# Two pairs of down blocks in each half by seven products of halves, and the output stored by fours of blocks

## The chip, the core and the metric

The kernel runs on one core of a Trainium2 chip. The metric is the device time of one execution in microseconds. The core's engines are named as in the profile: PE (matrix products) with PEld (its weight loads), DVE (vector operations), ACT (activations, scaling, casts), POOL (a second, slower vector engine, which here also issues some of the loads) and SP (which issues most loads and the stores).

## The reference

One layer of a decoder, for 256 prompt tokens and 8 sampled ones: half a SwiGLU block, a mixing block (a group of mLSTM heads beside a group of short convolutions), half a SwiGLU block, and a last norm.

```python
D_MODEL, SEQ, DEC_BATCH, D_FF = 2048, 256, 8, 5504

def swiglu(x, wg, wu, wd):
    return (jax.nn.silu(x @ wg) * (x @ wu)) @ wd

h = h + 0.5 * swiglu(rmsnorm(h, norm_ffn1), ffn1_gate, ffn1_up, ffn1_down)
h = h + mixing_block(rmsnorm(h, norm_mix), ...)
h = h + 0.5 * swiglu(rmsnorm(h, norm_ffn2), ffn2_gate, ffn2_up, ffn2_down)
y = rmsnorm(h, norm_final)
```

The change is in the products with `ffn1_down` and `ffn2_down` (5504 x 2048 each) and in how `y` leaves the chip.

## The kernel before

Tokens lie along the columns: all T = 264 of them, as 16 blocks `h[kb]` of 128 channels x 264. Every weight is cut into blocks of 128 x 128. Full precision is got from half-size numbers: a weight `w` becomes `hi + lo`, an activation likewise, and each block product is three matmuls, hi with hi, hi with lo, lo with hi (`three`, L287 to L289). `high` (ACT, L220) rounds to the high part, `low` (DVE, L228) takes what is left.

Weights are streamed in the order of one list, `weight_plan`. `fetch` takes the next chunk of up to 8 blocks: SP loads it into `wraw`, ACT writes `whi`, DVE writes `wlo`. `product` consumes the chunks in order and keeps AHEAD = 5 of them fetched. With `lag` set, the `low` of a chunk is issued only when the next chunk is fetched, so that DVE doesn't wait for ACT.

A SwiGLU layer (`ffn`) runs in two halves of the inner dimension, 22 and 21 blocks of 128. In each half come first the gate and up products of its blocks (16 k-blocks each), which leave the activations `act[j]` as high and low parts, then 16 down products (22 or 21 k-blocks), whose sums DVE adds to `h` (L846). After the second half of a layer each finished `h[db]` goes to `done`: in layer 1 that cuts it into parts for the mixing block and squares it, in layer 2 it squares it and applies the last gain. The squares (`square`) run on POOL.

Some gate/up blocks (`SEVEN`: 11 in layer 1, 12 in layer 2) go by seven products of halves. The two output blocks (gate and up), the two halves of the 16 k-blocks and the two halves of the tokens make a 2 x 2 by 2 x 2 product, for which seven products and some sums do in place of eight. One such pair costs

- four half loads of raw weights (`load`, issued by POOL, two buffers `sraw`), 
- the parts of three blocks as they are (`blocks` on ACT, `blocks_low` on DVE, tiles `sa`) and of four sums of blocks (`all_sums`, `sums_low`, tiles `sb`; three additions on DVE into `ssum`, L355 to L357),
- sums of the activations, the "forms" (`form` on POOL, `form_split` on ACT and DVE), made once for all pairs of a layer,
- 7 x 8 x 3 = 168 matmuls over 132 columns (`chunk_by_seven`, L409) in two chunks: three products, then four,
- the putting together of the results by DVE (`by_seven`, L759 to L763).

The preparation of the next pair is spread in eight steps over the ordinary products between two pairs (`prepare_step`, called after each chunk; `step_end` holds it back). `at(n, fn)` puts work off by n products (half products too): `tick` counts them. All engines take their instructions in the order in which the program issues them.

At the end the last two down blocks are made in two spans of tokens (136, then 128 columns), so that the first span's output is normed and stored while PE works on the second. `scaled` multiplies two blocks of `h` by the norm (L902) and stores them (L903). `watch` keeps sums of absolute values of the results, `judge_early` and `judge_late` compare them with bounds, and if one is outside, a branch repeats the whole step in full precision.

Of the kernel before, what the change touches and what calls it, by code (L numbers as in the profile page):

```python
# [8 lines left out]
F32 = mybir.dt.float32  # L9
# [40 lines left out]
SEVEN = {n: list(range(j, 22, 3)) + list(range(22, NFB, 3)) for n, j in (("1", 10), ("2", 7))}  # L50
PAIRS = sum(len(v) for v in SEVEN.values())
TH = T // 2
# [29 lines left out]

def weight_plan(a, apart=None):
# [10 lines left out]
    def ffn(layer, first):  # L94
        gu, d = a[f"w{layer}gu"], a[f"w{layer}d"]
        for half, blocks in enumerate(HALVES):
            for j in blocks:
                if j >= first and (apart is None or j not in apart[layer]):
                    add((layer, "g", j), gu[j, 0], KB)
                    add((layer, "u", j), gu[j, 1], KB)  # L100
            for db in range(KB):
                b0, b1 = blocks[0], blocks[-1] + 1
                add((layer, "d", half, db), d[db][:, b0:b1, :], b1 - b0)
# [42 lines left out]
def step(ctx: ExitStack, tc: tile.TileContext, a: dict, shared, bad=None):  # L146
# [7 lines left out]
    AHEAD = 5 if half_size else 2  # L154
    queue = nc.gpsimd if half_size else nc.sync
# [12 lines left out]
    hpair = []  # L168
    for kb in range(0, KB, 2):
        t = hpool.tile([128, 2, T], F32, name=f"h{kb}", tag=f"h{kb}")  # L170
        hpair.append(t)
        h += [t[:, 0, :], t[:, 1, :]]
# [144 lines left out]
    def prepare(pool, layer):  # L317
# [3 lines left out]
        gu = a[f"w{layer}gu"]  # L321
# [4 lines left out]

        def load(j, c):
            raws[c] = raw = pool.tile([128, 4, 4, 128], F32, tag="raw", name="sraw", bufs=2)
            for g in range(2):
                blocks = gu[j, g].rearrange("p (s k) m -> p s k m", s=2)  # L330
# [14 lines left out]
        sums = [None]  # L345

        def all_sums(j, c):
            raw = raws[c]
            if c == 0:
# [4 lines left out]
            sums[0] = s = pool.tile([128, 4, 4, 128], F32, tag="ssum", name="ssum")  # L354
            nc.vector.tensor_tensor(s[:, 2], raw[:, 2], raw[:, 3], op=ALU.add)  # L355
            nc.vector.tensor_tensor(s[:, 3], s[:, 2], raw[:, 1], op=ALU.subtract)
            nc.vector.tensor_tensor(  # L357
                s[:, 0:2], raw[:, 0:4:2],
                s[:, 3].unsqueeze(1).to_broadcast([128, 2, 4, 128]), op=ALU.subtract,
            )  # L360
            high(formed[j, 1][0][:, :, ks[c]], s, sw)

        def sums_low(j, c):
            hi, lo = formed[j, 1]
            low(lo[:, :, ks[c]], sums[0], hi[:, :, ks[c]], sw)

        for n, j in enumerate(SEVEN[layer]):
# [5 lines left out]
            for c in range(2):  # L373
                s = -4 if n == 0 else 8 * n + (-2, -1)[c]
# [8 lines left out]
    def chunk_by_seven(j, c, x, forms, banks):  # L383
# [3 lines left out]
        hi, lo = formed.pop((j, c))  # L387
        p, q, r = banks
        left, right = slice(0, TH), slice(TH, T)

        def form(n):
# [4 lines left out]
            (p, 1, lambda k: x[k][:, :, left]), (p, 0, lambda k: x[k + 8][:, :, left]),  # L396
            (r, 0, form(3)),
        )
        if c == 1:

            work = (
                (q, 0, lambda k: x[k][:, :, right]), (q, 2, form(1)), (q, 1, form(0)),
                (p, 2, form(2)),
            )
        for f, (ps, col, b) in enumerate(work):
# [7 lines left out]
            if f == 1:  # L413
# [157 lines left out]
    def judge(x, bounds):  # L571

        n = x.shape[-1]
        ok = tmp.tile([128, NSTAT], F32, tag="ok", name="ok", bufs=1)[:, :n]
# [50 lines left out]

    class Norm:
# [10 lines left out]
        def cut(self, kb):  # L637
# [10 lines left out]
            else:  # L648
                split(x, h[kb], gain)
# [3 lines left out]
        def form(self, k):  # L653


            b = tmp.tile([128, 7, TH], F32, tag="y7", name="form_b", bufs=1)
            t = tmp.tile([128, 4, TH], F32, tag="form_t", name="form_t", bufs=2)
# [5 lines left out]
            side.tensor_tensor(t[:, 0:2], b[:, 1:4:2], b[:, 0:2], op=ALU.subtract)  # L663
            side.tensor_tensor(t[:, 2], b[:, 3], t[:, 0], op=ALU.subtract)
            side.tensor_tensor(t[:, 3], t[:, 2], b[:, 2], op=ALU.subtract)
            self.parts = t

        def form_split(self, k):
            t = self.parts
            x = self.fpool.tile([128, 2, 4, TH], PART, tag=f"f{k}", name=f"f{k}")  # L670
            high(x[:, 0], t)
            self.forms.append(x)
            at(0.5 if seq[0] == int(seq[0]) else 1, low, x[:, 1], t, x[:, 0])
# [992 lines left out]
```

## Time and profile before

| | |
|---|---|
| median of 3 runs | 1816.19 us (1815.84 to 1818.47) |
| profiled execution | 1816.65 us; its span 1814.9 us |
| PE busy | 1797.8 us, 17918 matmuls |
| DVE busy | 1388.2 us, 2141 instructions |
| ACT busy | 953.1 us, 1329 instructions |
| POOL busy | 237.2 us, 338 instructions |
| granted clock of PE | 0.998 |
| moved by DMA | 381.34 MB |

The four down stages lie at about 243 to 362, 581 to 694, 1349 to 1468 and 1687 to 1786 us. In the timeline, times are counted from the start of the span. A row of a group gives its line, engine and operation, what it writes and reads, the shape, the count, then the busy time, the mean of one in ns, and the idle time of the engine before it with what ended it. In a row of a window the first number behind the colon is its length, then come the busy times.

### The profile page before, as it was taken

To read this page: it belongs to the slowest core of one execution; us is meant where nothing else is said; L and a number is where in the kernel's file an instruction comes from. 1 tells how busy PE (TensorE), PEld (TensorE's weight loads), DVE (VectorE), ACT (ScalarE), POOL (GpSimd) and SP (SyncE) were. 2 spreads that over 40 slices of the span, in tenths; PEclk is the share of its full clock that TensorE was granted. 3 is DMA by queue.
4 is the path that set the end of the run, shared out by engine and by line. 5 is a ranking of instruction groups with operands and counts; after the bars stand their busy time and mean duration, and the time that the engine had idled before them with its cause. 6 is when DMAs were issued, how large, how long until landed. Compare 5 with 4: busy or idle time off the path is not lost. (4 is left out here: it accounts for less than half of the span.)

```text
span 1814.9 us, 42526 instructions
## 1 busy us (share of the span) xinstructions
PE 1797.8 (99%) x17918; PEld 1591.0 (88%) x17918; DVE 1388.2 (76%) x2141; ACT 953.1 (53%) x1329; POOL 237.2 (13%) x338
## 2 busy tenths in 40 slices
PE   9999999999999999999999999999999999999997
PEld 7889988899998888888888888899988889999886
DVE  7888975579997657788888766789986459998564
ACT  7664554445554444567566645655554335554442
POOL 0310000000100222222121022410000001010110
PEclk9999999999999999999999999999999999999999
DMA  8665666645654565888887655756567646564553
GB/s 301 243 222 168 219 208 230 203 153 189 215 192 153 185 193 189 302 284 276 280 283 238 222 180 185 254 191 220 191 193 249 199 148 215 191 207 153 191 186 101
DMA packets 118615, 381.34 MB, mean 210 GB/s; under 512 B 15084, under 2 KB 24908, under 8 KB 118416
## 3 DMA queue, kind: packets, MB, share of 16 engines
q1 hardware_dynamic: 95952, 302.29, 50.1%
q0 software_dynamic: 21504, 75.81, 12.2%
q8 instruction: 142, 2.33, 0.5%
q10 hardware_dynamic: 960, 0.45, 0.1%
q14 instruction: 57, 0.47, 0.1%
HBM read 366.72 MB, written 11.78 MB: 209 GB/s over the span
## 5 line engine op out<-in xcount | busy, mean ns | idle before, releaser
L228 DVE SCALAR_TENSOR_TENSOR wlo<-wraw,whi 128x1024 f16<-128x1024 f32 (+2 forms) x600 | 688.2, 1172 | 103.5 <-ACT whi L220 102.9
L220 ACT ACTIVATE whi<-wraw 128x1024 f16<-128x1024 f32 (+2 forms) x600 | 580.0, 1000 | 160.6 <-PE ps L288 140.7
L289 PE MATMUL ps<-x,wlo 128*128 128x264 f16 x1952 | 538.8, 276 | 1.1 <-DVE wlo L228 1.1
L287 PE MATMUL ps<-x,whi 128*128 128x264 f16 x1952 | 538.8, 276 | 0.2 <-ACT whi L220 0.2
L288 PE MATMUL ps<-x,whi 128*128 128x264 f16 x1952 | 538.8, 276 | 0.0
L289 PEld LDWEIGHTS <-wlo 128*128 128x128 f16 x4522 | 442.5, 98 | 67.4 <-DVE wlo L228 2.4
L288 PEld LDWEIGHTS <-whi 128*128 128x128 f16 x4522 | 442.4, 98 | 66.2
L287 PEld LDWEIGHTS <-whi 128*128 128x128 f16 x4522 | 442.7, 98 | 65.6 <-issue 0.6
L289 PE MATMUL ps<-a,wlo 128*128 128x264 f16 (+2 forms) x1418 | 382.7, 273 | 0.4 <-DVE wlo L228 0.4
L287 PE MATMUL ps<-a,whi 128*128 128x264 f16 (+2 forms) x1418 | 382.8, 273 | 0.0
L288 PE MATMUL ps<-a,whi 128*128 128x264 f16 (+2 forms) x1418 | 382.8, 273 | 0.0
L287 PE MATMUL ps<-xm,whi 128*128 128x264 f16 x896 | 247.3, 276 | 0.0
L289 PE MATMUL ps<-xm,wlo 128*128 128x264 f16 x896 | 247.3, 276 | 0.0
L288 PE MATMUL ps<-xm,whi 128*128 128x264 f16 x896 | 247.3, 276 | 0.0
L220 ACT ACTIVATE sb<-ssum 128x2048 f16<-128x2048 f32 x46 | 87.9, 1911 | 181.2 <-DVE ssum L357 181.2
L409 PEld LDWEIGHTS <-sb 128*128 128x128 f16 x2208 | 128.8, 98 | 0.7
L846 DVE SCALAR_TENSOR_TENSOR h<-ps,h 128x264 f32<-128x264 f32 x62 | 26.7, 431 | 126.7 <-PE ps L289 126.7
L228 DVE SCALAR_TENSOR_TENSOR sb<-ssum,sb 128x2048 f16<-128x2048 f32 x46 | 105.2, 2288 | 8.0 <-ACT sb L220 5.6
L409 PE MATMUL ps<-f,sb 128*128 128x132 f16 x1656 | 99.0, 221 | 0.0
L409 PEld LDWEIGHTS <-sa 128*128 128x128 f16 x1656 | 97.1, 98 | 0.7
L331 POOL DMA_DIRECT2D sraw<-in_w2gu x48 | 34.6, 723 | 420.7 <-issue 371.5
L228 DVE SCALAR_TENSOR_TENSOR sa<-sraw,sa 128x1536 f16<-128x1536 f32 x46 | 81.8, 1778 | 3.1
(255 smaller groups left out, 1601.7 us busy)
## 6 DMA issues: line engine op xcount, KB each, us to landing
wraw<-in_w2gu SPq DMA_DIRECT2D x124, 512.0 KB, 4.6
wraw<-in_w1gu SPq DMA_DIRECT2D x120, 512.0 KB, 4.8
wraw<-in_win SPq DMA_DIRECT2D x112, 512.0 KB, 5.7
wraw<-in_w1d SPq DMA_DIRECT2D x80, 448.0 KB, 4.0
wraw<-in_w2d SPq DMA_DIRECT2D x80, 448.0 KB, 4.1
sraw<-in_w2gu POOLq DMA_DIRECT2D x48, 512.0 KB, 4.9
sraw<-in_w1gu POOLq DMA_DIRECT2D x44, 512.0 KB, 5.3
wraw<-in_wout SPq DMA_DIRECT2D x32, 512.0 KB, 4.8
```

The source lines that it names most:

```text
L220: nc.scalar.activation(dst, src, AF.Copy, scale=scale)
L228: nc.vector.scalar_tensor_tensor(dst, src, scale, hi, op0=ALU.mult, op1=ALU.subtract)
L287: nc.tensor.matmul(ps, wh, xk[:, 0, :], start=first, stop=False)
L288: nc.tensor.matmul(ps, wh, xk[:, 1, :], start=False, stop=False)
L289: nc.tensor.matmul(ps, wl, xk[:, 0, :], start=False, stop=last)
L331: queue.dma_start(raw[:, 2 * g : 2 * g + 2], blocks[:, :, ks[c], :])
L409: nc.tensor.matmul(out, w[:, f, k, :], b(k)[:, part, :], start=(k + term == 0), stop=(k == 7 and term == 2),)
L846: nc.vector.scalar_tensor_tensor(h[db], ps, 0.5 / (sw * sa[layer]), h[db], op0=ALU.mult, op1=ALU.add)
```

## The change

In each half of each layer the down blocks 6 and 7, and 10 and 11, go by sevens over the first 16 of the half's 22 or 21 k-blocks; the other 6 or 5 k-blocks of each are an ordinary product ("rest"). The order is written by `down_order`: ordinary products 0 to 5, then for a pair first chunk, an ordinary block, the first rest, second chunk, an ordinary block, the second rest.

Forms of the activations are made anew in each half: POOL adds the high and low parts of each block and makes three subtractions, ACT and DVE split the result. They start in the half's last gate/up block. The preparation of weights is paused from there until down block 3. The sums of weights are made in the buffers of the raw weights instead of `ssum`, and the load of the second half of the next pair is issued one step later. The down stages run with `lag` set.

The low parts of normed blocks (but of the first norm and the last block) are put off by one product. `judge_early` moves behind the last pair. The output is scaled and stored by four blocks, the last four by two and two: 4 stores for the first span and 5 for the second, where there were 8 and 8. Some temporary buffers change their pools or share one.

```diff
+SEVEN_DOWN = {"1": ((3, 5), (3, 5)), "2": ((3, 5), (3, 5))}
+def down_order(pairs, n):
+    order = []
+    for p in range(-(-n // 2)):
+        if p in pairs:
+            for c in range(2):
+                order += [("seven", p, c), ("one", 2 * p + 2 + c), ("rest", 2 * p + c)]
+        elif p - 1 not in pairs:
+            order += [("one", db) for db in range(2 * p, min(2 * p + 2, n))]
+    return order
...
@@ prepare
+            cut = slice(blocks_[0], blocks_[0] + KB)
+            for p in SEVEN_DOWN[layer][half]:
+                jobs.append((("d", half, p), d[2 * p][:, cut], d[2 * p + 1][:, cut]))
...
-            sums[0] = s = pool.tile([128, 4, 4, 128], F32, tag="ssum", name="ssum")
-            nc.vector.tensor_tensor(s[:, 2], raw[:, 2], raw[:, 3], op=ALU.add)
-            nc.vector.tensor_tensor(s[:, 3], s[:, 2], raw[:, 1], op=ALU.subtract)
+            nc.vector.tensor_tensor(raw[:, 3], raw[:, 2], raw[:, 3], op=ALU.add)
+            nc.vector.tensor_tensor(raw[:, 1], raw[:, 3], raw[:, 1], op=ALU.subtract)
             nc.vector.tensor_tensor(
-                s[:, 0:2], raw[:, 0:4:2],
-                s[:, 3].unsqueeze(1).to_broadcast([128, 2, 4, 128]), op=ALU.subtract,
+                raw[:, 0:4:2], raw[:, 0:4:2],
+                raw[:, 1].unsqueeze(1).to_broadcast([128, 2, 4, 128]), op=ALU.subtract,
             )
-            high(formed[j, 1][0][:, :, ks[c]], s, sw)
+            high(formed[j, 1][0][:, :, ks[c]], raw, sw)
...
-                s = -4 if n == 0 else 8 * n + (-2, -1)[c]
+                s = -4 if n == 0 else 8 * n + (-2, 0)[c]
...
+            def form(k):
+                b = form_blocks()
+                for n, i in enumerate((k + 8, k)):
+                    y = act[blocks[i]]
+                    side.tensor_tensor(
+                        b[:, 2 * n : 2 * n + 2].rearrange("p s t -> p (s t)"), y[:, 0, :],
+                        y[:, 1, :], op=ALU.add,
+                    )
+                forms.append(form_sums(b))
...
+                    if downs and j == blocks[-1]:
+                        paused, step_end[0] = step_end[0], min(step_end[0], step_no[0] + 1)
+                        for k in range(9):
+                            when = 2 + int(1.5 * k) / 2
+                            if k:
+                                at(when, form_split, k - 1)
+                            if k < 8:
+                                at(when, form, k)
...
+                def down_by_seven(p):
+                    y, halves = assemble(seven.pop(p))
+                    def summed():
+                        both = hpair[p].rearrange("p i t -> p (i t)")
+                        nc.vector.scalar_tensor_tensor(
+                            both, y[:, 0:4].rearrange("p s t -> p (s t)"), scale, both,
+                            op0=ALU.mult, op1=ALU.add,
+                        )
+                    at(1, halves)
+                    at(1, summed)
+                for kind, db, *c in down_order(downs, KB - apart):
+                    if kind == "seven":
+                        if c[0] == 0:
+                            seven[db] = [bank() for _ in range(3)]
+                        chunk_by_seven(("d", half, db), c[0], x, forms, seven[db])
+                        if c[0] == 1:
+                            down_by_seven(db)
+                        continue
+                    if downs and db == 3:
+                        step_end[0] = paused
+                    over = range(KB if kind == "rest" else 0, len(x))
+                    ps = product((layer, "d", half, db), x, over)
...
-        at(2 * NFB + 2 * KB - 8, judge_early)
+        more = 2 * sum(len(p) for p in SEVEN_DOWN["2"])
+        at(2 * NFB + 2 * KB + more - 2, judge_early)
...
-    for i in range(1 + half_size, NP):
-        scaled(i, cols, queues[i])
+    for k0, n, dma in ((8, 4, nc.sync), (12, 2, nc.scalar), (14, 2, nc.sync)):
+        scaled(k0, n, cols, dma)
```

More of the change, by code (lines that the diff above doesn't have):

```diff
@@ L325, in prepare @@
         step_no[0] = None
+        step_end[0] = 9
         def load(j, c):
@@ L648, in cut @@
             else:
-                split(x, h[kb], gain)
+                high(x[:, 0, :], h[kb], gain)
+                later = self.col != V_N1 and kb < KB - 1
+                (lambda *f: at(1, *f) if later else f[0](*f[1:]))(
+                    low, x[:, 1, :], h[kb], x[:, 0, :], gain
+                )
             self.x[kb] = x
@@ L662, in form @@
                 )
[L663 to L666, printed above, removed]
+            self.parts = form_sums(b)
         def form_split(self, k):
[L669 to L673, printed above, removed]
+            self.forms.append(form_parts(self.fpool, f"f{k}", self.parts))
         def square(self, kb):
```

151 lines of the change are left out of this document (94 added, 57 removed).

## The prediction

> **What bounds the kernel now.** I read the page first, then the list of waits on PE, then single stretches of the timeline, then the groups by shape.
>
> ```profile
> span 1814.9 us, 42526 instructions
> PE 1797.8 (99%) x17918; PEld 1591.0 (88%) x17918; DVE 1388.2 (76%) x2141; ACT 953.1 (53%) x1329; POOL 237.2 (13%) x338
> PEclk9999999999999999999999999999999999999999
> PE ps L962 <- DVE ok L956: 2.0, 1, 2.0
> PE ps L289 <- DVE wlo L228: 1.5, 3, 1.1
> ```
>
> PE is busy for 1797.8 of 1814.9 us at full granted clock, and the waits on it that the profile can name are one of 2.0 us at the very end and a few of about 1 us or less. So the time is the sum of the pitches of 17918 matmuls plus some 17 us of start, end and small gaps. Work on another engine costs nothing until it starves PE. The question is then what a matmul costs at the two widths involved: 264 columns in an ordinary product, 132 in a product by sevens.
>
> ```profile
> 27.91 0.28 PE L287 MATMUL ps<-x,whi 128*128 128x264 f16 x1
> ...
> 38.60 0.28 PE L289 MATMUL ps<-x,wlo 128*128 128x264 f16 x1
> ...
> 211.54 2.92 PE L409 MATMUL ps<-x,sa 128*128 128x132 f16 x48
> 214.30 1.54 PE L409 MATMUL ps<-f,sa 128*128 128x132 f16 x24
> 215.68 0.28 PE L287 MATMUL ps<-x,whi 128*128 128x264 f16 x1
> ```
>
> The first two rows are the first and last of 96 matmuls in a row: (38.60 - 27.91) / 95 = 112.5 ns from start to start (the 0.28 in a row is the latency of one, not its pitch). The last three hold 72 narrow ones between 211.54 and 215.68: 4.14 / 72 = 57.5 ns, with no gap where the width changes. Each has its own weight load, as the equal counts of PE and PEld on the page say.
>
> **The change, PE.** Sixteen of a half's 22 or 21 k-blocks of two output blocks cost 2 x 16 x 3 = 96 wide matmuls, 96 x 112.5 ns = 10.80 us. By sevens they are 7 products x 8 k-blocks x 3 terms = 168 narrow ones, 168 x 57.5 ns = 9.66 us. The "rest" products keep the other 6 or 5 k-blocks as they were. So one pair saves 1.14 us, and 8 pairs (two in each of two halves of two layers) save **9.1 us**. PE's count should be 17918 + 8 x 72 = 18494. This is the whole gain on offer; everything below asks what of it is lost.
>
> A rule speaks against it. The Trainium skill, page "TensorE: Matmul & The Clock Gate", section on the back-to-back issue gap, gives about 81 ns for each weight load and matmul at 128 columns and 131 ns at 512 in a real stream. By a line between those a pair would cost 168 x 81.5 = 13.7 us in place of 96 x 98.7 = 9.5 us, an estimate of 34 us lost over 8 pairs. The rows above, which are such a stream, have 57.5 and 112.5 ns, so I take theirs.
>
> **The change, DVE and ACT in a stretch with a pair.** The nearest row is one whole period of the gate/up stage, a pair beside four ordinary products, next to a whole down stage of before.
>
> ```profile
> core 0: us, PE busy (x) PEld busy (x) DVE busy (x) ACT busy (x) POOL busy (x), PEclk, DMA share, GB/s
> 444.96:476.22 31.26, 31.26 (x364) 28.45 (x361) 28.54 (x39) 16.62 (x19) 2.88 (x4) 1.00 0.60 200
> 581.00:694.30 113.30, 113.30 (x1011) 98.36 (x1009) 66.92 (x99) 47.16 (x65) 21.93 (x29) 1.00 0.61 195
> L228 DVE SCALAR_TENSOR_TENSOR wlo<-wraw,whi 128x1024 f16<-128x1024 f32 x420 | 508.6, 1227 | 51.8 <-ACT whi L220 51.5
> L228 DVE SCALAR_TENSOR_TENSOR wlo<-wraw,whi 128x896 f16<-128x896 f32 x160 | 170.3, 1094 | 48.9 <-ACT whi L220 48.9
> L836 DVE TENSOR_TENSOR tc<-ps,rstd 128x264 f32<-128x264 f32 x63 | 26.8, 426 | 15.0 <-PE ps L289 15.0
> L846 DVE SCALAR_TENSOR_TENSOR h<-ps,h 128x264 f32<-128x264 f32 x62 | 26.7, 431 | 126.7 <-PE ps L289 126.7
> L767 DVE TENSOR_TENSOR y<-y,rstd 128x528 f32<-128x528 f32 x23 | 16.3, 708 | 0.8
> L228 DVE SCALAR_TENSOR_TENSOR xm<-h,gains,xm 128x264 f16<-128x264 f32 x16 | 7.9, 494 | 9.3 <-ACT xm L220 9.3
> ```
>
> In that period DVE works 28.54 of 31.26 us and PE never stops. A down period with a pair has 9.66 us of sevens, two whole products (66 x 112.5 ns = 7.4 us in the first half, 63 x 112.5 = 7.1 in the second) and two rests (18 or 15 x 112.5 = 2.0 or 1.7): 28.6 and 27.2 us of PE. For DVE I swap the parts. Out go eight weight chunks of 1227 ns (9.8 us), the vector work of two ordinary blocks at four operations of 264 columns (8 x 0.43 = 3.4), and after the pair's sums the scaling and two gating operations (0.71 + 2 x 0.43). In come the chunks of two whole products and two rests (first half 4 x 1.09 + 2 x 1.23 + about 1.9 = 8.7, second half 6 x 1.09 + about 1.7 = 8.2, the rests by size from the 896 row), four evictions of 0.43 and one addition of 528 columns at 0.71 (`summed`). That is 28.5 - 14.8 + 11.1 = 24.9 us, 87% of the period in the first half; 24.4 us, 90%, in the second; and in layer 1's second half another 4 x 0.494 us for the low parts of the normed blocks, 26.4 us, 97%. The period that runs without a gap has 91%. Only one stretch goes above it, for one pair, since after the last pair no weights are prepared. Five chunks are kept ahead, 5 x 21 x 112.5 ns = 11.8 us of PE. So I put the cost of all this at 0; if the cover went, each us of DVE over the period would be a us of PE. ACT has 16.6 of 31.3 us there and stays far from its limit.
>
> **Sums in place** issue the same three additions; without `ssum` the buffer of raw weights is held one step longer, until `sums_low`, and the load that POOL issues for the next pair waits for that. In the period above:
>
> ```profile
> 466.22 2.28 DVE L228 SCALAR_TENSOR_TENSOR sb<-ssum,sb 128x2048 f16<-128x2048 f32 x1
> 473.67 1.47 ACT L220 ACTIVATE sa<-sraw 128x1536 f16<-128x1536 f32 x1
> 480.18 1.75 DVE L228 SCALAR_TENSOR_TENSOR sa<-sraw,sa 128x1536 f16<-128x1536 f32 x1
> sraw<-in_w1gu POOLq DMA_DIRECT2D x44, 512.0 KB, 5.3
> ```
>
> Freed at 468.5, loaded 5.3 us after the second of two issues of 0.7, the weights are there at about 474.5, some 1 us after ACT took them at 473.67. ACT would wait that us with its queue behind it; DVE takes the result only at 480.18. Hidden, cost 0 (bounds 0 and 2 us a half, if ACT's delay were passed on whole). On POOL nothing but forms and squares is queued behind the wait.
>
> **The forms of the activations** are new: eight a half, each two f16 additions and three subtractions on POOL, one split on ACT and DVE.
>
> ```profile
> L663 POOL TENSOR_TENSOR form_t<-form_b 128x264 f32<-128x264 f32 x16 | 13.0, 810 | 114.8 <-ACT form_b L659 94.0 <-DVE f L228 20.7
> L664 POOL TENSOR_TENSOR form_t<-form_b,form_t 128x132 f32<-128x132 f32 x16 | 12.6, 790 | 1.3
> L665 POOL TENSOR_TENSOR form_t<-form_t,form_b 128x132 f32<-128x132 f32 x16 | 14.8, 926 | 1.3
> L682 POOL TENSOR_TENSOR acc<-acc,sq 128x264 f32<-128x264 f32 x43 | 36.5, 849 | 3.4
> L678 POOL TENSOR_TENSOR sq<-h 128x264 f32<-128x264 f32 x43 | 26.9, 626 | 210.5 <-DVE h L846 83.3 <-DVE stat L537 74.1 <-DVE h L1567 53.1
> L228 DVE SCALAR_TENSOR_TENSOR f<-form_t,f 128x528 f16<-128x528 f32 x16 | 11.9, 742 | 0.0
> ```
>
> The f16 additions show in no row; rows of that size on POOL go from 0.63 to 0.85 us, and I take 0.81 (L663, also two operands). A form is then 2 x 0.81 + 0.81 + 0.79 + 0.93 = 4.15 us, eight are 33 us. They start in the last gate/up block and are wanted 2.8 us into the first pair, after one product of 5.4 us and six of 7.4 or 7.1: 52 or 50 us. In the second half POOL also has six squares (0.63 + 0.85 each) and four loads of 0.7 us, 45 us in all, and squares wait for their products. It fits with 5 to 15 us to spare: cost 0, DVE's eight splits (6 us over 50) included. With POOL reading beside it DVE is slower, by the next row, so I hold this against its margin as a rival.
>
> ```profile
> L228 DVE SCALAR_TENSOR_TENSOR wlo<-wraw,whi 128x1024 f16<-128x1024 f32 x10 | 13.0, 1319 | 1.2 <-ACT whi L220 1.2
> ```
>
> That is the stretch from 56 to 76 us, where POOL makes forms: 1319 ns in place of 1227. The Trainium skill, "SBUF — State Buffer", section on who interferes with whom, says that a DVE operation with two SBUF inputs and a reading GpSimd operation shut each other out; the 92 ns agree in sign, and a full lockout is not seen.
>
> **Starts of the down stages.** Two of the three waits for `wlo` on PE stand at 265 and 1371 us, at the first down products, where sums for the next pair compete with chunks. That work is now paused there. Each costs PE 0.2 us idle; I take back **0.4 us** (bounds 0 and 1).
>
> **The end.** `judge_early` moves from the middle of the last down stage to its last product.
>
> ```profile
> 1737.05 0.74 DVE L575 TENSOR_SCALAR ok<-stat 128x254 f32<-128x254 f32 x1
> ...
> 1741.08 3.08 DVE L228 SCALAR_TENSOR_TENSOR wlo<-wraw,whi 128x896 f16<-128x896 f32 x3
> ```
>
> It holds DVE for 4.0 us. Behind it now stand two evictions and the three chunks of the last block, while PE has only a rest (1.7 us) and one block at the first span (63 matmuls of 136 columns, a little over 57.5 ns each, some 3.7 us) to go: 5.4 us against 4.0 + 1.0 (chunk) + handing over, then another us for the next chunk. I take **+0.5 us** (bounds 0 and 2, the latter if DVE is already late).
>
> ```profile
> L902 DVE TENSOR_TENSOR h<-h,rstd 128x256 f32<-128x256 f32 x8 | 2.9, 419 | 0.0
> L903 SPq DMA_DIRECT2D out_yt<-h x13: 372/419/1847, 1797.4 to 1807.4; - x13
> DMA to landing us min/median/max: 1.8/3.0/4.5
> out_c_p<-co POOLq DMA_DIRECT2D x4, 257.0 KB, 5.6
> ```
>
> The last store starts at 1807.4 and can take 4.5 us, which sets the end. Scaling by fours takes five operations for the last span (three of 512 columns near the 0.71 of the 528 row, two of 0.42: 3.0 us) in place of eight (3.4). The last store keeps its size and has four fewer beside it. Landing could shorten to 1.8 us or, behind stores of 256 KB, lengthen as in the 5.6 row: from -2.7 to +1.1. I take **-0.2**, near the DVE difference, since bytes are the same.
>
> Retagged buffers and the low parts put off by one step issue nothing new: 0.
>
> **Sum.** -9.1 - 0.4 + 0.5 - 0.2 = -9.2 us. The profiled execution took 1816.65 us, 1.75 more than its span, and lies 0.46 above the median of 1816.19. So 1807.4 for a like execution and **1807.0** as the median; own range 1805.3 to 1809.5.
>
> **Rivals.** First, DVE becomes the bound in the pairs' stretches. For it: 97% in layer 1's second half, and 1319 against 1227 ns beside POOL; 90% grown by that 7.5% is 97%, and the 97% becomes 104%. Against it: the period with 91% and no gap, and 11.8 us kept ahead. If each of the 8 pairs lost half its 1.14 us, 4.6 us go and the time is 1811.6: 1809.5 to 1814, chance 10%.
>
> Second, the other side: forms come late. PE would stand in the third product of each first pair. The point is some 5 us of slack in the second halves: a form of 4.8 us there. At additions of 2.5 us (a form of 7.5) eight take 60 us plus 1.4 for loads against 52, 9 us lost in each of four halves and more in the second ones, so 1807 + 36 = 1843 or slower. For it: f16 operands on POOL show nowhere, and one row's mean is 0.93 for half the size. Against it: no POOL operation of this size has a mean above 0.85. Chance 5%.
>
> Third, the weight loads of the narrow matmuls are not hidden with these operands.
>
> ```profile
> L409 PEld LDWEIGHTS <-sb 128*128 128x128 f16 x2208 | 128.8, 98 | 0.7
> ```
>
> At 98 ns each a pair would take 168 x 98 = 16.5 us in place of 10.8, 45 us more over 8 pairs, 1861. Against it: 2208 such loads cover only 128.8 us, 58 ns each, since they overlap. 1%. (The issue-gap rule above is of this kind.) Last, the change does not do what it says: the guard's sums for the new pairs fall outside their bounds and the whole step runs again in full precision, at least another 1800 us. 2%; the sums are of the same kind as those of the 23 pairs of before, after which the span ends at once.
>
> **Numbers.** Forecast 82%, rivals 10, 5, 1 and 2%. About 0.2%, 3.6 us, is what can be told from no change: faster is below 1812.6, so the forecast and three quarters of the first rival, 0.89; same 0.04; slower 0.07. The range runs from 1805.3 (0.8 us at the starts and 1 us at the end won) into the first rival, 1811.5.
>
> **What would show it.** PE x18494 and its busy time near 1788.7; 168 narrow matmuls a pair without gaps in the four down stages; DVE near 1490 us, POOL near 390; no PE wait on `f` (forms late), few on `wlo`, `sa` or `sb` (else DVE is the bound); a `wlo` wait under 1 us near the end. Waits of PE on `wlo` or `sa`/`sb` inside the down stages, over 3 us in all, would make the prediction wrong.

## Result and profile after

The changed kernel took **1874.55 us** (median of 6 runs, 1871.72 to 1876.27) where the one before took 1817.16 beside it: a ratio of **1.0314 [1.0303, 1.0324]**. Forecast were 1807.0 us (1805.3 to 1811.5). The page of the profiled execution (1872.74 us):

```profile
span 1870.9 us, 43912 instructions
PE 1807.1 (97%) x18494; PEld 1597.5 (85%) x18494; DVE 1525.6 (82%) x2262; ACT 990.3 (53%) x1369; POOL 440.0 (24%) x530
PEclk9999999999999999999999999999998999999999
```

PE has the 18494 matmuls foreseen, but is busy for 9.3 us more than before instead of 9.1 less, and its idle time grows from 17.1 to 63.8 us. What PE waits for (engine, line, result, releaser: us, times, longest):

```profile
PE ps L310 <- DVE wlo L249: 36.7, 24, 3.3
PE ps L437 <- DVE sb L249: 5.3, 3, 2.7
PE ps L308 <- ACT a L241: 3.4, 2, 2.0
PE ps L1059 <- DVE ok L1053: 2.3, 1, 2.3
PE ps L437 <- DVE fa L249: 1.1, 1, 1.1
```

The forms are late for their pair once, by 1.1 us. Nearly everything is `wlo`: the low parts of ordinary weight chunks. The 3.4 us for `a` stand where a down stage begins: at 252 us PE stops for 2.0 us for the last activation, which ACT had behind a form that it stood 4.8 us for. Two stretches at the starts of the down stages, first of before and then of after (columns as in the prediction's windows; the last three are the granted clock, the DMA share and GB/s):

```profile
248.00:300.00 52.00, 51.79 (x462) 44.81 (x460) 34.75 (x44) 23.67 (x24) 2.88 (x4) 1.00 0.72 243
600.00:650.00 50.00, 50.00 (x447) 43.48 (x446) 29.79 (x43) 21.25 (x28) 10.65 (x14) 1.00 0.60 196
```

```profile
248.00:300.00 52.00, 41.85 (x354) 34.68 (x352) 41.94 (x44) 24.20 (x29) 44.12 (x44) 0.97 0.54 161
600.00:650.00 50.00, 42.18 (x364) 34.53 (x362) 42.20 (x45) 22.35 (x30) 42.03 (x45) 0.97 0.57 176
290.00:300.00 10.00, 5.51 (x37) 3.83 (x35) 9.97 (x10) 6.88 (x8) 7.10 (x6) 0.83 0.56 186
```

PE loses 10 and 8 us in a stretch that has no pair yet. In the first, DVE did 44 instructions in either kernel, not the same ones (seven splits of forms are among those of after), and was busy 41.94 us in place of 34.75; the low part of a 128x896 chunk, which both have, took 1342 ns in place of 1084. In the last row DVE is full while PE does half its work, at a granted clock of 0.83: the clock fell in a stop of PE of 3.3 us. Over the span such drops add up to 23.9 us at half clock, each 3.4 us long or a multiple (near 294, 638, 1331, 1420, 1430 and 1775 us); before had none until the very end. POOL's forms in the first half:

```profile
L832 POOL TENSOR_TENSOR form_b<-a 128x264 f32<-128x264 f16 x16 | 16.9, 1078 | 16.5 <-DVE a L249 16.0
L662 POOL TENSOR_TENSOR form_t<-form_b 128x264 f32<-128x264 f32 x8 | 9.5, 1188 | 2.8 <-DVE fa L249 2.3
L663 POOL TENSOR_TENSOR form_t<-form_b,form_t 128x132 f32<-128x132 f32 x8 | 8.4, 1046 | 0.6
L664 POOL TENSOR_TENSOR form_t<-form_t,form_b 128x132 f32<-128x132 f32 x8 | 7.4, 920 | 0.6
```

A form takes 2 x 1.08 + 1.19 + 1.05 + 0.92 = 5.3 us, not 4.15. By stage (a stage runs from the first matmul that reads its activations to the first of the next one), in us against the same stage of before; "1a" is the first half of layer 1, "2b" the second half of layer 2, and runs 1 to 16 are the experiments below. Each row is one profiled execution, which lies up to 3.3 us above the median of its kernel:

| kernel | gate/up 1a | down 1a | gate/up 1b | down 1b | mix | gate/up 2a | down 2a | gate/up 2b | down 2b, end |
|---|---|---|---|---|---|---|---|---|---|
| after | +1.7 | +12.4 | 0 | +9.7 | +0.4 | +6.9 | +13.0 | 0 | +11.6 |
| 1 no pairs | +2.8 | +11.2 | 0 | 0 | 0 | +6.7 | +10.9 | 0 | -1.0 |
| 2 no forms | +3.5 | -0.6 | 0 | -2.3 | +1.4 | +8.1 | +0.6 | 0 | -0.4 |
| 3 forms on DVE | +2.1 | +9.7 | 0 | +10.1 | 0 | +10.7 | +10.2 | 0 | +8.9 |
| 4 third step later | -0.5 | +11.5 | 0 | +11.6 | 0 | 0 | +11.6 | 0 | +13.6 |
| 5 spread | 0 | 0 | 0 | +6.2 | +5.0 | 0 | +1.7 | 0 | +4.5 |
| 6 splits only | +1.4 | +1.3 | 0 | -2.3 | +1.1 | 0 | +0.6 | 0 | +0.9 |
| 7 POOL beside | +1.3 | +6.0 | 0 | +5.0 | +1.4 | 0 | +9.3 | 0 | +14.6 |
| 8 stores only | 0 | 0 | 0 | 0 | 0 | 0 | 0 | 0 | -1.1 |
| 9 no pairs, paused | -0.6 | +3.6 | 0 | 0 | 0 | 0 | +2.0 | 0 | -1.1 |
| 10 one pair | +0.4 | -1.5 | 0 | 0 | 0 | 0 | -1.5 | 0 | -0.7 |
| 11 four single | +1.1 | -1.5 | 0 | +5.6 | +5.9 | 0 | -1.5 | 0 | +7.1 |
| 12 one, crowded | +1.0 | +9.8 | 0 | 0 | 0 | +0.6 | +11.8 | 0 | -0.7 |
| 13 stand later | -0.1 | +5.4 | +7.3 | +14.6 | 0 | 0 | +7.6 | +9.6 | +13.7 |
| 14 four, stand later | +1.4 | -1.5 | +7.8 | +3.4 | +4.5 | +1.4 | -1.5 | +14.1 | +10.4 |
| 15 none, stand later | +1.4 | -0.4 | +12.4 | 0 | 0 | +0.8 | -0.4 | +9.3 | -1.1 |
| 16 one, stand later | -0.1 | -1.5 | +15.3 | 0 | 0 | +0.7 | -1.5 | +10.9 | -0.6 |

So 46.7 us are lost in the four down stages and 8.6 in the two first gate/up stages. A theory was formed for each: in the down stages POOL's forms crowd DVE; in gate/up the later load of raw weights is late for ACT. A rival for the first was that the pairs themselves overload DVE or PE.

### The profile page after: what moved, and what is told of

Read it like the earlier page. It is cut to its first block, busy times and chain, and to the rows that moved or that the text cites. A ratio compares the mean times of both kernels' runs of the same rounds, so it can differ in the third digit from the quotient of the medians.

```text
span 1870.9 us, 43912 instructions
## 1 busy us (share of the span) xinstructions
PE 1807.1 (97%) x18494; PEld 1597.5 (85%) x18494; DVE 1525.6 (82%) x2262; ACT 990.3 (53%) x1369; POOL 440.0 (24%) x530
## 4 chain that ended last, share of the span: by engine, by line
PE 64%; DVE 15%; ACT 6%; issue 5%; POOL 5%; DMA 4%; ACTq 0%; DVEq 0%; POOLq 0%; SPq 0%
PE ps L310 17%; PE ps L308 17%; PE ps L309 17%; PE ps L437 11%; DVE wlo L249 4%; ACT sb L241 2%; POOL form_b L832 2%; ACT whi L241 2%; DVE sraw L384 2%; DMA sraw<-in_w2gu 2%; DVE sraw L383 1%; DMA sraw<-in_w1gu 1%; DVE sraw L382 1%; DVE sb L249 1%; DVE sa L249 1%
## 5 line engine op out<-in xcount | busy, mean ns | idle before, releaser
L249 DVE SCALAR_TENSOR_TENSOR wlo<-wraw,whi 128x1024 f16<-128x1024 f32 (+4 forms) x568 | 678.0, 1214 | 82.1 <-ACT whi L241 81.5
L241 ACT ACTIVATE whi<-wraw 128x1024 f16<-128x1024 f32 (+4 forms) x568 | 548.9, 996 | 74.6 <-PE ps L309 40.0
L309 PEld LDWEIGHTS <-whi 128*128 128x128 f16 x4266 | 418.7, 98 | 67.6 <-issue 4.0
L308 PEld LDWEIGHTS <-whi 128*128 128x128 f16 x4266 | 419.0, 98 | 65.0 <-ACT whi L241 2.9
L310 PE MATMUL ps<-a,wlo 128*128 128x264 f16 (+2 forms) x1162 | 316.8, 276 | 35.6 <-DVE wlo L249 35.6
L308 PE MATMUL ps<-a,whi 128*128 128x264 f16 (+2 forms) x1162 | 316.6, 276 | 4.8 <-ACT a L241 3.4
L309 PE MATMUL ps<-a,whi 128*128 128x264 f16 (+2 forms) x1162 | 316.6, 276 | 1.4 <-DVE a L249 1.4
L241 ACT ACTIVATE sb<-sraw 128x2048 f16<-128x2048 f32 x62 | 118.5, 1911 | 219.6 <-DVE sraw L384 219.6
L437 PEld LDWEIGHTS <-sb 128*128 128x128 f16 x2976 | 175.2, 98 | 6.7 <-DVE sb L249 5.8
L249 DVE SCALAR_TENSOR_TENSOR sb<-sraw,sb 128x2048 f16<-128x2048 f32 x62 | 145.0, 2339 | 34.6 <-ACT sb L241 33.7
L437 PEld LDWEIGHTS <-sa 128*128 128x128 f16 x2232 | 130.9, 98 | 3.1 <-issue 1.2
L241 ACT ACTIVATE sa<-sraw 128x1536 f16<-128x1536 f32 x62 | 91.3, 1473 | 43.1 <-DMA sraw<-in_w2gu 21.3
```

The lines of the kernel that those rows point to most:

```text
L241: nc.scalar.activation(dst, src, AF.Copy, scale=scale)
L249: nc.vector.scalar_tensor_tensor(dst, src, scale, hi, op0=ALU.mult, op1=ALU.subtract)
L308: nc.tensor.matmul(ps, wh, xk[:, 0, :], start=first, stop=False)
L309: nc.tensor.matmul(ps, wh, xk[:, 1, :], start=False, stop=False)
L310: nc.tensor.matmul(ps, wl, xk[:, 0, :], start=False, stop=last)
L437: nc.tensor.matmul(out, w[:, f, k, :], b(k)[:, part, :], start=(k + term == 0), stop=(k == 7 and term == 2),)
```

## Experiments

Each ratio is to the kernel before as it ran beside (1816.2 to 1817.2 us).

**Run 1: no down pairs.** `SEVEN_DOWN = {"1": ((), ()), "2": ((), ())}`.

> No down block goes by sevens; the sums in place, the later second load, the stores by fours and the deferred low parts stay. Theory (the gate/up stages lose by the weights arriving late, whatever the down stages do): the loss of 8.6 us that the trace after shows in the first halves' gate/up stages (+1.7 in layer 1, +6.9 in layer 2) stays, so about 1826 us, with ACT's waits for the second load (3 to 5 us each) still there. Rival (those stages lose only because the down jobs and their forms crowd them): no loss, 1817 us.

1846.19 us (1844.33 to 1847.83), ratio 1.0158 [1.0141, 1.0175]. The total meets neither forecast; the stages tell more. The gate/up loss stayed (+2.8, +6.7), as the theory says, so it has nothing to do with pairs. But the first down stages lost 11 us without any. In layer 1 PE stops for 2.5 us at 251 and 4.1 us at 257, the second time for the last activation, which ACT had behind its wait of 5.75 us for DVE's sums. The pause of the preparation, which keeps the sums away from there, went out with the pairs; run 9 puts it back. The kernel before has no pause and loses 0.2 us there: its last activation is done at 244 us, ahead of the first sums' stand, which ends at 252. So another part of the change has a hand in it; which one was not told apart.

**Run 2: no forms.** The output differs: the sevens read the norm's forms.

```diff
-  for k in range(9): ... at(when, form_split, k - 1) ... at(when, form, k)
+  forms.extend(norm.forms)
```

> The down pairs run, but the forms of the activations are left out: the pairs read the gate/up stage's forms in their place (same tiles' shape, other numbers). Theory (forms on POOL are what starves PE in the down stages): the four down stages fall from +46.7 us to about -9 us against before, so 1874.5 - 56 = about 1819 us, the rest being the gate/up stages' loss. Rival (DVE is the bound through the pairs' weights): the down stages keep most of their loss, 1855 us or more.

1826.15 us (1822.93 to 1826.9), ratio 1.0041 [1.0027, 1.0056]. The down stages go from +46.7 to -2.7 us: their loss is the forms', POOL's part and the splits together. About -9 was expected; only down 1b has its -2.3 us, two pairs at the 1.14 forecast.

**Run 3: forms on DVE.** The five additions and subtractions of a form go to DVE, three forms half a product later.

```diff
-  side.tensor_tensor(b[:, 2 * n : 2 * n + 2]..., op=ALU.add)
+  nc.vector.tensor_tensor(b[:, 2 * n : 2 * n + 2]..., op=ALU.add)
-  at(when, form, k)
+  at(when + 0.5 * (k in (3, 5, 7)), form, k)
```

> The forms' additions and subtractions are made by DVE in place of POOL, three of the eight half a product later so that DVE does not wait for itself. DVE gets some 8 x 1.9 = 15 us more a half. Theory (POOL's slowness, its blocking of DVE and ACT's waits behind it cost, not the work itself): 1835 us (1824 to 1850). Rival (DVE's total load in these stretches is the bound): no better than the changed kernel, 1875 us or above.

1865.5 us (1862.77 to 1868.52), ratio 1.0261 [1.0244, 1.0278]: between the two. It doesn't tell them apart, since DVE is then filled by the forms themselves: 50.51 of 52 us from 248 on. There is no room for forms on either engine at this pace.

**Run 4: the parts of the second half load one step later.** The load itself stays where the change put it; ACT and DVE cut its blocks into parts (steps 3 and 4 before) one step later.

```diff
-  (2, blocks, 0), (3, blocks_low, 0), (3, blocks, 1), (4, blocks_low, 1),
+  (2, blocks, 0), (3, blocks_low, 0), (4, blocks, 1), (5, blocks_low, 1),
```

> The parts of the second half load (ACT and DVE) are made one step later, as the load itself was moved one step; everything else as changed. Theory (ACT stands at the head of its queue for weights that have not landed): the gate/up stages of the first halves lose their 8.6 us, about 1866 us. Rival (the late load is hidden and those gaps have another cause): 1874 us.

1864.48 us (1864.22 to 1864.56), ratio 1.026 [1.0243, 1.0277], as expected: the gate/up losses are gone (-0.5, 0). The waits and the tile's rows of after say what it was:

```profile
ACT sa L241 <- DMA sraw<-in_w2gu: 21.3, 8, 5.9
ACT sa L241 <- DMA sraw<-in_w1gu: 14.7, 7, 6.2
L361 POOL DMA_DIRECT2D sraw<-in_w2gu x2: 722/723/724, 1295.4 to 1296.1; - x2
L241 ACT ACTIVATE sa<-sraw x2: 1470/1476/1482, 1297.6 to 1305.0; 128x1536 f16<-128x1536 f32 x2
```

The second load is issued by 1296.8, ACT gets it at 1305.0, after standing 4.9 us with the weight chunks behind it; DVE's `sa` and `sb` come late, and PE stops for 0.8, 2.7 and 1.2 us near 1312, 1328 and 1363. This kernel is the base of what follows.

**Run 5: pairs later, forms spread** over 8 products in place of 6, seven pairs (on run 4).

```diff
-SEVEN_DOWN = {"1": ((3, 5), (3, 5)), "2": ((3, 5), (3, 5))}
+SEVEN_DOWN = {"1": ((4, 6), (4, 6)), "2": ((4, 6), (4,))}
-  when = 2 + int(1.5 * k) / 2
+  when = 2 + k
```

> On top of the third-load edit (1864.5 us): the pairs lie one pair later (blocks 8, 9 and 12, 13; in the very last stage only 8, 9), and the forms are spaced one product apart, so that they have some 67 us in place of 50; seven pairs in place of eight. Theory (forms, sums of weights and the low parts crowd DVE, ACT and POOL in the first 50 us of each down stage): the loss a stage falls from 11.6 us to 3 or less, 1815 to 1832 us. Rival (each form costs PE its part wherever it lies): about 12 us a stage stay, 1860 us or more.

1833.97 us (1832.39 to 1837.36), ratio 1.0099 [1.0082, 1.0115]: 30 us are won back, all 11.5 of down 1a and most of 2a; in the second halves a loss stays. Pace, place and number of the pairs changed together here; run 12 takes the pace alone.

**Run 6: the splits without POOL** (on run 4). The output differs: the forms are views of `h`, split by ACT and DVE as before.

```diff
-  (the additions and form_sums of form(k))
+  forms.append(hpair[k].rearrange("p i (s t) -> p (i s) t", s=2))
```

> On top of the third-load edit: POOL makes no forms; ACT and DVE split two blocks of the residual (tiles of the same size) in their place, so their own work stays and the results differ. Theory (POOL's part costs): like the kernel without forms, but without the gate/up loss, 1813 to 1819 us. Rival (the 16 splits on ACT and DVE are what is too much): 1840 us or more.

1817.03 us (1816.03 to 1819.65), ratio 1.0005 [0.9995, 1.0014]. POOL's part is worth 47 us, the splits little.

**Run 7: POOL's forms beside.** As run 6, and POOL makes its forms, which nobody reads (so the output differs in the same way).

```diff
   forms.append(hpair[k]...)
+  b = form_blocks()
+  (the additions and form_sums(b) of form(k))
```

> As the kernel that splits the residual, but POOL makes all its additions and subtractions beside, and nobody reads their result (the results differ in the same way). Nobody waits for POOL then; what is left of its cost is that it slows DVE. Theory A (DVE slowed by POOL): most of the loss comes back, 1840 us or more. Theory B (ACT waits at the head of its queue for POOL's result): no loss, at most 1822 us.

1851.97 us (1850.58 to 1854.16), ratio 1.0192 [1.0175, 1.0209]: **35 of the 47 us are lost again though nothing waits for a form.** The groups on DVE from 248 to 300 us, first of run 6, then of run 7:

```profile
L249 DVE SCALAR_TENSOR_TENSOR wlo<-wraw,whi 128x896 f16<-128x896 f32 x12 | 13.1, 1088 | 0.4 <-ACT whi L241 0.4
L249 DVE SCALAR_TENSOR_TENSOR wlo<-wraw,whi 128x1024 f16<-128x1024 f32 x7 | 8.6, 1222 | 2.3 <-ACT whi L241 2.3
L384 DVE TENSOR_TENSOR sraw<-sraw 128x1024 f32<-128x1024 f32 x2 | 2.4, 1224 | 0.1
248.00:300.00 52.00, 51.43 (x493) 45.04 (x491) 40.81 (x49) 25.96 (x29) 2.88 (x4) 1.00 0.68 224
```

```profile
L249 DVE SCALAR_TENSOR_TENSOR wlo<-wraw,whi 128x896 f16<-128x896 f32 x13 | 17.7, 1369 | 0.0
L249 DVE SCALAR_TENSOR_TENSOR wlo<-wraw,whi 128x1024 f16<-128x1024 f32 x6 | 9.8, 1630 | 0.0
L384 DVE TENSOR_TENSOR sraw<-sraw 128x1024 f32<-128x1024 f32 x2 | 3.2, 1620 | 0.1
248.00:300.00 52.00, 48.13 (x448) 41.30 (x446) 49.14 (x48) 22.71 (x25) 46.47 (x39) 0.97 0.58 175
```

The same operations take 26, 33 and 32% longer beside POOL; DVE goes from 40.81 to 49.14 us with an instruction less. The prediction had 1319 against 1227 ns, 7.5%, from a stretch where POOL worked 7.78 of 20 us. PE's busy time tells the clock's share: 1790.0 us in run 6 and 1804.6 in run 7 for the same 18494 matmuls, 14.6 of the 35 us, beside 30.7 us at half clock.

Against run 6 the four down stages lose 4.7, 7.3, 8.7 and 13.7 us. In the first three no engine waits for POOL, so DVE's slowing, with whoever stands behind DVE, is what is left. In the last, 2b, theory A doesn't hold alone: ACT, which applies the last gain to each finished block, waits there for POOL's square of that block, and the squares stand in POOL's queue between the forms. Run 6, then run 7 (total, times, longest):

```profile
ACT h L985 <- POOL sq L721: 31.5, 12, 4.9
```

```profile
ACT h L993 <- POOL sq L721: 39.8, 12, 9.0
```

ACT gets going again at 1746.6 us after those 9.0, with the next chunk's high part behind, and PE stops for 3.5 us until 1748.0 for it; DVE is busy for only 35.66 of the 50 us from 1714 on.

**Run 8: only the stores by fours** on the kernel before (`scaled`, `hfour` and the end as in the change).

> The kernel before with only the output by fours (9 stores, five scalings of the last span in place of eight). In the run without pairs the last stage ended 1.0 us earlier with this part and the moved judge_early together. Theory: it is the stores alone, 1815.2 us (ratio 0.9993 to 0.9997). Rival: the earlier end came from something else in that run and the stores bring what the prediction put, 0.2 us or less: 1816.0 or more.

1815.67 us (1814.85 to 1817.04), ratio 0.9994 [0.9985, 1.0003]. The runs can't tell this from nothing; in the profile the last stage is 1.1 us shorter and no other differs.

**Run 9: no pairs, but the pause** (on run 4).

```diff
+SEVEN_DOWN = {"1": ((), ()), "2": ((), ())}
-  if downs and j == blocks[-1]:
+  if half_size and j == blocks[-1]:
-  for k in range(9):
+  for k in range(9 if downs else 0):
-  if downs and db == 3:
+  if half_size and db == 3:
```

> As the kernel with the loads' third step put later, with no pair of down blocks at all, but with the preparation of weights by sevens paused from a half's last gate/up block to its fourth down block, also where there is no pair. Theory: the 11 us that the run without pairs lost in each first down stage came from that missing pause, so they are gone here and what is left is the kernel before with a shorter end: 1814 to 1817 us. Rival: something else in the rest of the change (sums in place, the low parts a step later, shared buffers) takes that time: 1830 or more.

1821.46 us (1820.42 to 1823.74), ratio 1.0028 [1.0017, 1.0039]: between the two and nearer to the theory. +3.6 and +2.0 us stay in the first down stages, with no form made. ACT's list of times from 262 us on:

```profile
271.53 1.91 ACT L241 ACTIVATE sb<-sraw 128x2048 f16<-128x2048 f32 x1 [6.00 <-DVE sraw L384]
273.34 0.93 ACT L241 ACTIVATE whi<-wraw 128x896 f16<-128x896 f32 x1
280.22 1.91 ACT L241 ACTIVATE sb<-sraw 128x2048 f16<-128x2048 f32 x1 [5.95 <-DVE sraw L384]
282.04 4.51 ACT L241 ACTIVATE whi<-wraw 128x896 f16<-128x896 f32 x5
```

The preparation of the next pair, which the pause put here, makes ACT stand twice at `sb` (behind DVE's sums) with one weight chunk between; a chunk feeds PE for 21 x 112.5 ns = 2.4 us, and five in store last 11.8. The kernel before has two such stands as well (6.1 and 5.7 us, until 262 us), but two chunks between, and PE loses 0.2 us there.

**Run 10: one pair in each first half,** the seventh, its forms over 11 products in place of 6 (`when` runs from 2 to 13, not to 8; the expectation counts 12); the pause in every half (on run 9).

```diff
+SEVEN_DOWN = {"1": ((6,), ()), "2": ((6,), ())}
-  when = 2 + int(1.5 * k) / 2
+  when = 2 + int(2.8 * k) / 2
```

> As the run with no pair but the pause, plus one pair (7) in the first half alone of each layer, its forms on POOL stretched over 12 products (2 + 1.4 k) in place of 6. If POOL's forms cost only where they crowd DVE, the two pairs keep their 1.14 us each: 2.3 us below the run with no pair, about 1812.5. If a form costs DVE the same time wherever it stands and DVE has no room for it, the two stages give 2 to 6 us back: 1815 to 1820.

1813.65 us (1812.45 to 1815.87), ratio **0.9983 [0.9974, 0.9992]**: the one version here that beats the kernel before, by 0.17%, at the edge of what can be told.

```profile
span 1811.6 us, 42901 instructions
PE 1795.0 (99%) x18062; PEld 1591.1 (88%) x18062; DVE 1431.6 (79%) x2174; ACT 965.1 (53%) x1347; POOL 335.6 (19%) x426
```

Each first down stage is 1.5 us shorter: 1.14 for the pair, as forecast, and 0.4 for the start, where 0.2 was forecast for each.

**Run 11: one pair in each half** (on run 10; pace 2 + 1.1 k in the last).

```diff
+SEVEN_DOWN = {"1": ((6,), (6,)), "2": ((6,), (5,))}
```

> The run with one pair in each first half (1813.65 us), plus one pair in each second half: pair 6 in layer 1 with the same pace of forms (2 + 1.4 k), pair 5 in layer 2 with 2 + 1.1 k, since its last two blocks are taken apart. If the pace is all that counts, each brings another 1.14 us: 1811 to 1812. If the second halves have no room (POOL has the sums of squares there, DVE the low parts of the normed blocks), they give it back: 1814 to 1822.

1831.42 us (1828.39 to 1836.04), ratio 1.0078 [1.0065, 1.0091]. The first halves keep their 1.5 us; the second ones have no room at this pace either. From 581 us on:

```profile
581.00:640.00 59.00, 55.22 (x467) 46.54 (x466) 53.64 (x59) 28.75 (x40) 46.11 (x42) 0.94 0.57 175
```

POOL is busy 46.11 of 59 us, squares among it, and DVE 53.64.

**Run 12: one pair, forms crowded again** (run 10 with `when = 2 + int(1.5 * k) / 2`).

> The run with one pair in each first half, the forms alone moved back to the pace of the changed kernel (2 + 0.75 k, over 6 products in place of 12); the pair stays the seventh. If POOL's crowding of the first 50 us is what costs, PE loses several us in each of the two stages even though no product waits for a form: 1820 to 1836. If it was the early pair that waited for its forms, and the second pair's weights, and not the pace, nothing is lost: 1812 to 1815.

1836.1 us (1834.35 to 1839.22), ratio 1.0101 [1.0087, 1.0116]. The pace alone takes 22 us. The decisive rows, 248 to 300 us, 265 to 285 us and ACT's wait at the sums from 240 to 300 us, run 10 and then run 12:

```profile
248.00:300.00 52.00, 52.00 (x465) 45.22 (x463) 45.26 (x50) 25.48 (x29) 32.41 (x30) 1.00 0.69 229
265.00:285.00 20.00, 20.00 (x180) 17.39 (x178) 18.42 (x20) 10.33 (x10) 2.58 (x4) 1.00 0.57 192
ACT sb L241 <- DVE sraw L384: 9.1, 2, 4.9
```

```profile
248.00:300.00 52.00, 45.44 (x364) 37.09 (x362) 45.03 (x47) 24.32 (x29) 39.50 (x38) 0.90 0.53 167
265.00:285.00 20.00, 17.64 (x144) 14.50 (x142) 15.93 (x14) 7.55 (x9) 14.89 (x16) 0.92 0.41 126
ACT sb L241 <- DVE sraw L384: 13.0, 2, 8.0
```

In run 10 POOL works 2.58 us there: it waits to issue the loads, whose buffers come free only after the sums, and its forms queue behind. In run 12 they run beside the sums, 14.89 us; ACT stands 8.0 us, PE stops and its clock falls. Over the whole 52 us DVE is as busy in run 10 as in run 12, and its low parts of 128x896 are as slow (1302 and 1279 ns), yet PE loses nothing in run 10. So DVE's slowing by itself doesn't cost here; what costs is its slowing at the sums, where ACT stands with PE's chunks behind it.

**Runs 13 to 16: ACT's stand shortened.** ACT's high parts of the sums go one chunk behind the sums, the low parts one more, in run 4 (13), 11 (14), 9 (15) and 10 (16); the loads go a chunk later too. ACT's longest stand there from 240 to 300 us goes from 8.0 to 5.3 us in run 13 and from 6.0 to 3.7 in run 15.

```diff
-  (5, all_sums, 0), (6, sums_low, 0), (7, all_sums, 1), (8, sums_low, 1),
+  (5, all_sums, 0), (6, sums_high, 0), (7, sums_low, 0), (7, all_sums, 1),
+  (8, sums_high, 1), (9, sums_low, 1),
-  8 * n + (-2, 0)[c]
+  8 * n + (-1, 1)[c]
```

> The kernel with the loads' third step put later (1864.48 us: two pairs a half, forms crowded), but ACT's high parts of the sums of blocks issued one chunk after DVE's sums and DVE's low parts one chunk after that, loads one chunk later, so that ACT doesn't stand at the sums with its weight chunks queued behind it (it stood there 8.0 and 5.0 us beside the forms, 4.9 and 4.3 in the run with one pair that lost nothing). Theory S: this stand, made longer by POOL, is where most of the down stages' 47 us goes: 1820 to 1845. Theory D: DVE slowed by POOL and ACT's stands at the forms do it, wherever the high parts stand: 1855 or more.

1875.51 us (1871.85 to 1877.87), ratio 1.0323 [1.0307, 1.0339].

> The run with one pair in each of the four halves (1831.42 us) with the same shift of the high and low parts. Theory S: the second halves keep their pairs, 1811 to 1818. Theory D: 1826 or more.

1857.29 us (1856.51 to 1860.28), ratio 1.023 [1.0216, 1.0244].

> The run with no pairs but the pause (1821.46 us) with the same shift. It makes no forms, and lost 3.6 and 2.0 us in the first down stages, where ACT stood 6.00 and 5.95 us at the sums with one weight chunk between. Theory S: that loss goes, 1814.5 to 1816.5. If the stand is not its cause: 1820 or more.

1835.55 us (1833.64 to 1838.8), ratio 1.01 [1.0085, 1.0116].

> The run with one pair in each first half (1813.65 us) with the same shift. Both theories: 1812.5 to 1814.5, since nothing was lost there; above 1816 the shift itself costs (loads land a chunk later, the raw buffers are held longer).

1838.3 us (1835.21 to 1840.22), ratio 1.0114 [1.0099, 1.013].

All four totals missed theory S, and would read as theory D for three of them; run 16, where both theories expected no change, shows that the shift itself costs. The totals decide nothing, because the loads, a chunk later, are now late in the second gate/up stages (+7 to +15 us each). The wait that does it, of run 15:

```profile
PE ps L440 <- DVE sb L249: 11.4, 9, 1.5
PE ps L440 <- DVE sa L249: 8.3, 6, 2.5
```

The down stages, which the shift was aimed at, do tell. With no forms the loss goes entirely (+3.6 and +2.0 become -0.4 and -0.4). With crowded forms a third to a half of it goes in the first halves (+11.5 and +11.6 become +5.4 and +7.6), and nothing in the second ones (+11.6 and +13.6 become +14.6 and +13.7). So ACT's stand at the sums carries at least that much of the first halves' loss. The rest wasn't divided: DVE's slowing elsewhere, the stand that is left and, by run 7 against run 4, up to 12.5 us in all from those who wait for a form. What holds the second halves is told in part by run 7's trace: in 2b ACT's waits for POOL's squares, in 1b a DVE that is busy for 57.41 of the 60 us from 590 on.

## Why the prediction was wrong

- **PE, -9.1 us: right.** With POOL's part out (run 6) PE is busy 1790.0 us against 1788.7 forecast; a pair brings 1.14 us (down 1b of runs 2 and 6, run 10). The issue-gap rule that the prediction set against its rows is not what this chip did here.
- **Forms, 0: the step that failed, by 47 us** (run 4 against run 6). Two things went into it. The price: 5.3 us a form, not 4.15, since the f16 additions took 1.08 us and not 0.81, and the first two subtractions 1.19 and 1.05 and not 0.81 and 0.79. By that alone forms would be late for their pair, the second rival; PE waited 1.1 us for them. The other was the step from "it fits" to cost 0: POOL's time was held against POOL's deadline, not against what POOL does to DVE while it works. DVE, forecast near 1490 us, took 1525.6, and 1495.6 for as many instructions once POOL's part was out (run 6). A row for what POOL does to DVE was in the prediction, 1319 against 1227 ns, and was held against the pairs' periods alone; the forms run in the 50 us ahead of the first pair, where DVE makes the sums for the next one and ACT stands behind it. The average over a POOL that was busy 39% of the time looked mild; beside a busy POOL DVE's operations grow by 26 to 33% (run 7), and one shape on POOL takes 462 ns at its fastest and 2393 at its slowest. The rule cited there (the Trainium skill, "SBUF — State Buffer", section on who interferes with whom: the ports that the two engines share are an exclusive lock) was set aside as "a full lockout is not seen"; these rows are nearer to it than that stretch was.

```profile
L663 POOL TENSOR_TENSOR form_t<-form_b,form_t x8: 462/1000/2393, 251.1 to 294.9; 128x132 f32<-128x132 f32 x8
```

- **Pairs' periods, 0: right as such, but some 3 us are lost behind them in each first half.** In run 6 PE doesn't stop from the first pair's start at 289 us to 354 us. It stops for 0.6 us at 286, before the pair, and for 1.1 and 1.7 us at 354 and 358, after the last pair's matmuls have ended at 337. There DVE makes the sums for the first pair of the next gate/up stage, which PE reaches at 364.6 us, and ACT stands 6.8 and 4.3 us behind them. The prediction's "after the last pair no weights are prepared" holds for layer 1's second half, whose pairs came in full even at 97%, and not for the first halves.
- **Later load, 0 (0 to 2 us a half): 8.6 us.** The prediction saw ACT some 1 us late and called it hidden. ACT stood 3 to 6 us in several pairs, up to 6.2; in the case shown the landing came 8 us after the second issue, where the prediction took 5.3.
- **Starts, -0.4 (0 to 1): twice that,** 0.4 in each of the two stages, and only where nothing crowds them (runs 10, 15, 16).
- **judge_early, +0.5 (0 to 2): about +2.** It held DVE for 4.7 us in place of 4.0, and PE stops for 0.8, 0.6 and 0.8 us at 1844 to 1848 us, between the last products. Runs 9 and 10 move it too, but end on whole products, and show no stop there. The wait for `ok` at the end is 2.3 us, before's 2.0.
- **Stores, -0.2: -1.1** in the profile, inside the bounds.
- **Missing altogether: the clock.** 23.9 us at half clock cost about 12 us, an estimate by the half that is missing; so a stop can cost more than itself. The Trainium skill, "TensorE: Matmul & The Clock Gate", section on HAM oscillation, says that a wait of PE that crosses the activity window of some 3.4 us puts it back to half rate. The trace agrees in the length of the drops, 3.41 and 6.83 us, and shows them after shorter stops too; the last section has the numbers.

The sign that would make the prediction wrong was named rightly, waits on `wlo`, `sa` or `sb` in the down stages over 3 us; there were over 35.

## What to carry to other kernels

Work on a helper engine is not free when its own deadline is met: price it also by what the others lose while it runs, from a row where it is busy all the time, in the stretch where it will run. Look there for an engine that stands in order behind another (here ACT behind DVE's sums) with PE's food queued behind it, and give the helper a pace that leaves that place alone: with the forms spread over 11 products the same pair paid in full, over 6 it cost 11 us. And a change to a shared schedule is read by stages: in runs 13 and 15 the stages aimed at got better and the total worse.

## What was not expected of the hardware

- A DVE operation of 128x896 with two SBUF inputs took 1088 ns alone and 1369 beside a POOL busy 46.47 of 52 us (runs 6 and 7); one of POOL's 132-column subtractions took 462 to 2393 ns in the changed kernel.
- POOL's sum of two f16 tiles of 128x264 into f32 took 1078 ns in the mean beside a busy DVE (682 at the fastest), longer than any f32 row of that width before (849).
- When a stop halves the clock can be read off the trace. The six drops of the changed kernel begin at 293.61, 638.36, 1331.26, 1420.01, 1430.25 and 1774.99 us, which is 101, 304, 330, 333 and 434 steps of 3.413 us after the first. In the step just before a drop PE stood still for 2.2 to 2.8 us; in all others (from 60 us on, the end left out) for 1.74 at most. So a stop of 2.26 us at 1417.0, which lies within one step, is followed by half clock, and one of 2.25 us at 282.3, which is spread over two, is not. The profiles of the other runs have such a grid too, each its own; drops follow 1.8 us or more, and steps without one reach 2.0. Two drops, at 1420 and 1430, lie in this stretch:

```profile
1416.00:1440.00 24.00, 17.51 (x133) 13.09 (x132) 23.32 (x25) 12.57 (x14) 12.81 (x12) 0.79 0.57 200
```
